# Low weight parts on VectorE, small scalings on ScalarE, and the second chunk's norm as urgent work, in the first phase of a two-layer convolution and pooling trunk

## The chip, the cores and the metric

The kernel runs on one core of a Trainium2 chip. A core has TensorE (PE: matrix products, results in eight PSUM banks), VectorE (DVE), ScalarE (ACT), GpSimd (POOL) and SyncE (SP, which here only starts DMA transfers); PEld is the loading of weights into TensorE. Each engine takes its own instructions in order, and the engines wait for each other by semaphores. The metric is the device time of one execution in microseconds (us); the median of several runs counts.

## The reference

Two residual layers on x of 1024 positions by 1024 channels. Each sub-layer is an RMS norm, a shift and a scale computed from a conditioning vector c (adaLN), the sub-layer's work, a gate and the residual sum. Layer 0 mixes tokens by a Conformer convolution, layer 1 by pooling over trailing windows; a SwiGLU block follows each. The part that the change touches is the start of layer 0:

```python
c_act = jax.nn.silu(c)
mod = c_act @ ada_w[i] + ada_b[i]                  # six vectors of 1024
sh_m, sc_m, g_m, sh_f, sc_f, g_f = jnp.split(mod, N_ADA, axis=-1)
h = rms_norm(x, norm_mix_g[i]) * (1.0 + sc_m) + sh_m
u = h @ w1 + b1                                    # 1024 -> 2048
a, g = jnp.split(u, 2, axis=-1)
u = a * jax.nn.sigmoid(g)
u = causal_depthwise_conv(u, w_dw) + b_dw          # width 31, per channel
u = jax.nn.silu(layer_norm(u, ln_g, ln_b))
y = u @ w2 + b2
x = x + (1.0 + g_m) * y
```

All data is float32, and the products must have float32's precision.

## The kernel before, in words

**Layout.** Channels lie on the 128 partitions in KT = 8 tiles, positions on the free axis. The 1024 positions are two chunks of 512: A is x[0], B is x[1]. A is worked on ahead of B, and B's convolution input reuses the last 30 columns of A's (`uhalo`).

**Products in three parts.** A float32 operand is split into a high part in the fast type fp32r and a low part, the rest. `products` (L416) multiplies high by high, high by low and low by high. One product of a weight tile with 512 columns is one matmul; a half tile ("a" or "g", 8 channel tiles times 3 parts) is 24 matmuls, a tile 48. `load_weight` (L402) makes the two parts of a weight tile of 128x1024: a DMA into `raw` (4 buffers), the high part by a cast on ACT, and the low part in one of two ways. Without `summed` it is raw - high by a TENSOR_TENSOR on DVE or POOL, whichever `either` (L151) reckons free first by the planner's clocks and prices. With `summed` ACT writes the negated high rounding and a DMA from POOL's queue adds the source to it. High and low parts share nine buffers of the tag "w" (W_BUFS), in which the first phase also keeps its modulation weights.

**First phase** (L1270 to L1375). For each channel tile k of A: two rows of the modulation matrix (`ada_pair`, L1300) come in by DMA; two dot products on DVE with silu(c) (`ada_dot`, a SCALAR_TENSOR_TENSOR with an accumulator, tile `adaw`) give the scale's and the shift's column of tile k; `gain_of` (L1310) turns the first into the norm's gain (`gains`, one column) and a TENSOR_SCALAR adds the bias to the second (`mod`), both on DVE. Then t = x * gain * 1/rms on DVE, hhi = t + shift on ACT (fp32r), hlo = the rest on DVE one round later. The weights of the first FIRST = 4 tiles of w1 for this k are one tile of 128x1024 (`w1k`), split by `load_weight` with `either`. PE multiplies: 8 matmuls each of high weight by hhi, low weight by hhi, high weight by hlo, into the eight banks `first`. So there are eight rounds of 24 matmuls. The order on DVE is bound by hand with `behind_that` (L1306); the order of the loads on SP by `load_next` (L144), which chains each load to the one before.

Behind the rounds the two weights of tile 4 are loaded and split (`early`, L1378), then all eight tiles of x for B are loaded (L1379). `conv_glu` (L579) empties the eight banks: a sigmoid on ACT, a product on DVE, `u`.

**Units, tasks and the planner.** What follows is a list of units that `run_units` (L537) emits in order: products on PE, in the order written, and loads of weights ahead of them as buffers allow. Work of the other engines is cut into tasks (L208), generators that `pace` (L185) steps each time a quarter of a tile (12 matmuls) has been emitted. The planner keeps a clock per engine: 512 columns of a matmul count 0.216 us, an operation on DVE or POOL its price. A step of an urgent task is emitted at normal priority and as soon as its time has come; a step of another task only while DVE's or POOL's clock is less than 4 us ahead of PE's, at a lower priority, and behind the products emitted so far (`step`, L175). A task may ask to be left alone for a time, in the planner's us (LOAD, L50): "late" 11.0, "load" 4.8. Within an engine the final order comes from the tool that schedules by priority and its own timing; only PE keeps the written order.

**The units here.** In this order (L1417 on): `ada_first` starts `ada_columns` (L359), which computes the other four modulation vectors of layer 0 on PE. It loads rows in pairs (2 x 512 KB) into two buffers, waits "late" ahead of the first pair and "load" ahead of the others, multiplies (`ada`, 8 matmuls a row), and loads the next pair; sixteen pairs in all. Then the task `norm_b` (L1424): B's eight squares on ACT summed on DVE into a PSUM bank (`Squares`, L462), the sum over partitions by 8 small matmuls (`var`), three Newton steps for the root on DVE (`mean_rsqrt`, L437), its spreading by 8 matmuls (`rstd`), and for each of eight tiles t, hhi and hlo (`modulated`, L509). It is not urgent and stands at the front of the task list. Then the convolution's taps for A's tiles 0 to 3: tap by tap on DVE (`ca`, in PSUM) or on ACT and POOL (`pr`, `pa`). Then tile 4 of A; then tiles 5 and 6 of A, `finish(norm_b)`, and tiles 5 and 6 of B with the same weights; then tile 7 of both, tiles 0 to 3 of B, A's layer norm, the second product `y`, and so on to the feed-forward parts.

Of the kernel before, what the change touches and what calls it, by code (L numbers as in the profile page):

```python
# [9 lines left out]
F32 = mybir.dt.float32  # L10
F32R = mybir.dt.float32r
I32 = mybir.dt.int32
AF = mybir.ActivationFunctionType
ALU = mybir.AluOpType
MUL, ADD, SUB = ALU.mult, ALU.add, ALU.subtract

P = 128
D = 1024
S = 1024
KT = D // P  # L20
# [20 lines left out]
FIRST = 4  # L41
# [5 lines left out]
PHTAPS = 29  # L47
PHLEN = 135
OUT_B = 3
LOAD = {"load": 4.8, "late": 11.0, "slow": 18.0, "next": 4.0}  # L50
AHEAD = 4
STRETCH = 1.35
LATER = 300
WARM = (22, 10, 6)
PREPARED = 120
PLAIN = 4
UNTIL = (16, 16, 20)
# [55 lines left out]
def trunk(ctx, tc, xT, c, vec, ada, adan, w1, w2, wgu, wdn, wpl, wph, out):  # L113
    nc = tc.nc
    ctx.enter_context(tc.manual_schedule(engines={mybir.EngineType.PE}))
    clock = {"PE": 0.0, "V": 0.0, "G": 0.0, "S": 0.0}
    V_ = Engine(nc.vector, "V", clock, PRICES["V"], lambda i: order(i))
    G_ = Engine(nc.gpsimd, "G", clock, PRICES["G"], lambda i: order(i))
    S_ = Engine(nc.scalar, "S", clock, PRICES["S"], lambda i: order(i))
# [11 lines left out]
    def order(ins):  # L131

        if behind[0] and last_mm[0] is not None:
            tc.add_manual_dep(ins.ins, last_mm[0], edge, reason="behind the products")
        return ins
# [8 lines left out]
    def load_next(dst, src):  # L144

        d = nc.sync.dma_start(dst, src)
        if last_load[0] is not None:
            tc.add_manual_dep(d.ins, last_load[0], edge, reason="loads in order")
        last_load[0] = d.ins.name

    def either(n):  # L151

        now = clock["PE"]
        v, g = (max(clock[e], now) + engines[e].price("tensor_tensor", n) for e in "VG")
        return V_ if v <= g else G_
# [9 lines left out]
    def nm(s):  # L165
        uid[0] += 1
        return f"{s}_{uid[0]}"
# [40 lines left out]
    class Task:  # L208
# [6 lines left out]
        def step(self, e):  # L215
            if e != "V" or self.done or clock["PE"] < self.until and not forced[0]:
                return False
            try:
# [3 lines left out]
                if said == "wait":  # L222
                    return False
                if said in LOAD:
                    self.until = clock["PE"] + LOAD[said]
                elif said is not None:
# [18 lines left out]
    def bank(name):  # L245
        return ps.tile([P, 512], F32, tag="mm", name=nm(name))
# [27 lines left out]
    x = [[cst.tile([P, ch.n], F32, name=f"x_{ch.i}_{k}") for k in range(KT)] for ch in chunks]  # L274
# [21 lines left out]
    def V(name, j, n=1):  # L296
        b = _COLS[name] + j
        return vecs[:, b : b + n]

    mod = cst.tile([P, DEPTH * 6 * KT], F32, name="mod")  # L300
    gains = cst.tile([P, 4, DEPTH * KT], F32, name="gains")
    scale_m, scale_f, gate_m, gate_f = (gains[:, i] for i in range(4))
# [96 lines left out]
        return mod[:, b : b + 1]  # L399


    def load_weight(src, n=D, load=nc.sync.dma_start, summed=False):  # L402
        raw = raws.tile([P, D], F32, tag="raw", name=nm("raw"))[:, :n]
        as_src = lambda t: t if len(src.shape) == 2 else t.rearrange("p (a b) -> p a b", a=src.shape[1])
        load(as_src(raw), src)
        hi, lo = (wts.tile([P, D], F32R, tag="w", name=nm("w"))[:, :n] for _ in range(2))
        S_.copy(hi, raw)
        if summed:
            S_.activation(lo, raw, AF.Copy, scale=-1.0)
            order(nc.gpsimd.dma_start(as_src(lo), src, accum_op=ADD))  # L410
            clock["G"] = max(clock["G"], clock["PE"]) + 1.0
            return hi, lo
        either(n).tensor_tensor(lo, raw, hi.bitcast(F32), op=SUB)
        return hi, lo

    def products(out, wt, k, act, first, last, o=0, n=None):  # L416
# [117 lines left out]
    def unit(emit, *weights):  # L534
        units.append((weights, emit))
# [138 lines left out]
    class Phased:  # L674
# [5 lines left out]
        def load(self):  # L680
            self.w = []
            for g in range(PH):
                for h in range(2):
                    t = slot(A, "wph", F32)
                    nc.sync.dma_start(t, wph[self.i, g][:, h * 512 : h * 512 + 512])
                    self.w += [t[:, m * P : m * P + P] for m in range(SHIFTS // 2)]
# [301 lines left out]
    class Pair:  # L988
# [15 lines left out]
        def prepare(self):  # L1004
# [10 lines left out]
            def fresh():  # L1015
                t = wts.tile([P, D], F32R, tag="w", name=nm("w"))
                return t[:, FRONT], t[:, BACK]
# [3 lines left out]

            with tc.high_priority(offset=-PREPARED):
                w11, w12, w22 = fresh(), fresh(), fresh()
# [30 lines left out]
    class Downs:  # L1054
# [13 lines left out]
        def load(self, dp):  # L1068
# [5 lines left out]
            wt = wts.tile([P, D], F32R, tag="w", name=nm("w")).rearrange("p (s f d) -> p s f d", s=2, f=2)  # L1074
            with tc.high_priority(offset=-PREPARED):
                S_.copy(wt[:, 0], raw)
# [212 lines left out]
    summed = V_.last.ins.name  # L1289
# [4 lines left out]
    S_.activation(ccols[:, :, 0], V("c", 0, KT), AF.Silu)  # L1294
    scale_b = cst.tile([P, KT], F32, name="scale_b")
    G_.tensor_scalar(scale_b, V("ada_b", KT, KT), 1.0, None, op0=ADD)
    ada_m = ada.rearrange("(l j k) p d -> l k p j d", l=DEPTH, j=6)
    w1k = w1[0:FIRST].rearrange("a b p (k m) -> k p (a b) m", k=KT)

# [6 lines left out]
    def behind_that(name, reason):  # L1306
        tc.add_manual_dep(V_.last.ins, name, edge, reason=reason)
        return V_.last.ins.name

    def gain_of(k):  # L1310
        V_.tensor_scalar(scale_m[:, k : k + 1], mod[:, KT + k : KT + k + 1], scale_b[:, k : k + 1], V("norm_mix_g", k), op0=ADD, op1=MUL)

    warm(WARM[0])
    b = bank("var")
# [4 lines left out]
    ada_dot(w[1], 0, 1, 0)  # L1319
    at = behind_that(summed, "while the tensor engine sums")  # L1320
    gain_of(0)
    at = behind_that(at, "in order")
    v, t = b[:, :count], b[:, 16 : 16 + count]
    V_.tensor_scalar(v, v, EPS, None, op0=ADD)
    at = behind_that(at, "in order")
    col = tmp.tile([P, 16], F32, tag="col1", name=nm("col"), bufs=1)[:, :count]
    now(rsqrt(v, col, t))
    rooted = V_.last.ins.name
    warm(WARM[1])
    r = bank("rstd")  # L1330
    for i in range(count):
        matmul(r[:, i * P : (i + 1) * P], col[:, i : i + 1].broadcast_to([P, P]), ident, start=True, stop=True)
    warm(WARM[2])
    rstd_a = temp(A.n, "ny", 2)
    h_a = st["h", 0] = [(slot(A, "hhi"), slot(A, "hlo")) for _ in range(KT)]
    fb = [bank("first") for _ in range(BANKS)] + [spare_bank("first") for _ in range(2 * FIRST - BANKS)]
    for k in range(KT + 1):
        if 0 < k < KT:
            w = ada_pair(k)
            ada_dot(w[1], 0, 1, k)  # L1340
            behind_that(lo_last if k == 1 else t_last, "behind the tile ahead of it")
        if k > 0:
            dot = V_.last.ins.name
            if k > 1:
                V_.scalar_tensor_tensor(h_a[k - 1][1], t, mod[:, k - 1 : k], h_a[k - 1][0].bitcast(F32), op0=ADD, op1=SUB)
                if k < KT:
                    behind_that(dot, "the scalar engine's part takes that long")
            for i, (wp, a) in enumerate(((0, 0), (1, 0), (0, 1))):
                for q in range(2 * FIRST):
                    matmul(fb[q], wt[wp][:, q * P : (q + 1) * P], h_a[k - 1][a], start=k == 1 and i == 0, stop=k == KT and i == 2)  # L1350
        if k < KT:
            ada_dot(w[0], 0, 0, k)
            if k == 0:
                behind_that(rooted, "while the root is spread")
            else:
                gain_of(k)
            V_.tensor_scalar(mod[:, k : k + 1], mod[:, k : k + 1], V("ada_b", k), None, op0=ADD)
            t = temp(A.n)
            V_.scalar_tensor_tensor(t, x[0][k], scale_m[:, k : k + 1], rstd_a if k else r, op0=MUL, op1=MUL)
            t_last = V_.last.ins.name  # L1360
            S_.activation(h_a[k][0], t, AF.Identity, bias=mod[:, k : k + 1])
            if k:
                wt = load_weight(w1k[k], 2 * FIRST * P, load_next)
            else:
                first_hi = S_.last.ins.name
                raw = raws.tile([P, D], F32, tag="raw", name=nm("raw"))
                load_next(raw.rearrange("p (a b) -> p a b", a=2 * FIRST), w1k[0])
                wt = [wts.tile([P, D], F32R, tag="w", name=nm("w")) for _ in range(2)]
                S_.copy(wt[0], raw)
                S_.copy(rstd_a, r)  # L1370
                tc.add_manual_dep(S_.last.ins, first_hi, edge, reason="the first tile reads the bank")
                V_.tensor_tensor(wt[1], raw, wt[0].bitcast(F32), op=SUB)
                at = behind_that(t_last, "in order")
                V_.scalar_tensor_tensor(h_a[0][1], t, mod[:, 0:1], h_a[0][0].bitcast(F32), op0=ADD, op1=SUB)
                lo_last = behind_that(at, "in order")  # L1375
    for e in clock:
        clock[e] = max(clock.values())
    early = [load_weight(w1[FIRST, i], load=load_next) for i in range(2)]  # L1378
    for k in range(KT):  # L1379
        load_next(x[1][k], xT[:, k, B.t0 : B.t0 + B.n])  # L1380
    for p in range(FIRST):
        conv_u(A, p)
        conv_glu(A, p, fb[2 * p], fb[2 * p + 1])
# [2 lines left out]
    T = {}  # L1386
# [31 lines left out]
    def norm_first():  # L1418
        squares = Squares(B, True)
        for k in range(KT):  # L1420
            squares.add(k)
            yield
        yield from norm(B, 0, False, ("h", 1), squares=squares)
    unit(lambda take: T.__setitem__("norm_b", Task(norm_first(), False, 0)))  # L1424
    taps(A, *range(FIRST))
    for p in range(FIRST, SHARED[0]):
        conv_in((A, p))
# [158 lines left out]
```

## Time and profile before

| | before |
|---|---|
| three runs, us | 1834.56, 1834.21, 1831.17; median 1834.21 |
| the profiled execution | 1831.12, its span 1829.3 |
| mean granted clock of TensorE | 0.992 |
| busy: PE, DVE, ACT, POOL | 1781.2, 1309.1, 1028.8, 589.2 us |
| moved by DMA | 340.63 MB, 186 GB/s on average |

The chain of work that ended last lies on PE for 80% of the span, on DVE for 8% and on DMA for 6%.

How to read it: a row of the timeline gives the start and the length of a run of equal instructions in us from the span's start, then engine, line, operation, out<-in with the programs' names, and in brackets how long the engine had stood idle just before and who released it. Nearly all operations are recorded in a helper (L107, L129), so the tile names tell them apart. A row of the stages gives a stretch, its length, the busy us (and instructions) of PE, PEld, DVE, ACT and POOL, PE's granted clock, the busy share of the DMA engines and GB/s. A row of the groups has busy us, the mean ns of one instruction, and the idle time ahead of it with its releasers. Matmuls overlap by their pipeline, so the distance of two starts is what one costs PE.

### The profile page before, as it was taken

Reading aid. Unit: us, or ns where it says so; the run is one execution under the profiler, and the core shown is the slowest. Engines: PE = TensorE matmul, PEld = TensorE weight load, DVE = VectorE, ACT = ScalarE, POOL = GpSimd, SP = SyncE. Lnnn points to the kernel's source line nnn. Section 1 sums busy time; section 2 is a strip of 40 time slices with the busy share of each in tenths; the row PEclk is TensorE's granted clock in tenths of the full one; section 3 lists DMA queues with packets and bytes.
Section 4 is the critical chain, followed back from the end, with each engine's and each line's share of the span. In section 5 each row is a group of like instructions: output and inputs, shape, how many; then the busy total and the mean of one; then the engine's idle time right before and its main releaser. Section 6 shows DMA issues by size and latency. Waiting matters only on the chain.

```text
span 1829.3 us, 26250 instructions
## 1 busy us (share of the span) xinstructions
PE 1781.2 (97%) x9748; PEld 1519.4 (83%) x9748; DVE 1309.1 (72%) x2136; ACT 1028.8 (56%) x1590; POOL 589.2 (32%) x632
## 2 busy tenths in 40 slices
PE   8989999999999999999999999999999999999997
PEld 7756678888888887899997888999978889999986
DVE  8878754988766237889978458778694468887845
ACT  3655575866756455655545456555554546555543
POOL 2578722877743211311117121111151211011111
PEclk9989999999999999999999999999999999999998
DMA  8838869798887997976767887655568876655462
GB/s 271 279 116 258 228 153 216 198 234 210 221 232 181 242 223 179 255 216 199 207 179 160 203 182 169 156 139 138 145 147 201 181 167 159 189 141 135 130 141 70
DMA packets 115377, 340.63 MB, mean 186 GB/s; under 512 B 11441, under 2 KB 21809, under 8 KB 115250
## 3 DMA queue, kind: packets, MB, share of 16 engines
q1 hardware_dynamic: 76656, 222.56, 36.4%
q0 software_dynamic: 37440, 115.36, 35.2%
q8 instruction: 76, 1.25, 0.3%
q10 hardware_dynamic: 1154, 1.05, 0.2%
q14 instruction: 51, 0.42, 0.1%
HBM read 334.73 MB, written 4.19 MB: 185 GB/s over the span
## 4 chain that ended last, share of the span: by engine, by line
PE 80%; DVE 8%; DMA 6%; issue 3%; POOL 2%; ACT 2%; SPq 0%; POOLq 0%; DVEq 0%; ACTq 0%
PE gate L129 23%; PE up L129 23%; PE dn L129 22%; PE y L129 5%; DMA adaw<-in_adan_dram 3%; PE a L129 2%; PE g L129 2%; DVE t L107 1%; DVE adaw L107 1%; DMA w<-in_wdn_dram 1%; DVE hlo L107 1%; DVE x L107 1%; DVE win L107 1%; DMA w<-in_wgu_dram 1%; PE ada L129 1%
## 5 line engine op out<-in xcount | busy, mean ns | idle before, releaser
L129 PE MATMUL dn<-ghi,w 128*128 128x512 f32 (+1 forms) x1440 | 468.8, 388 | 3.4 <-DMA w<-in_wdn_dram 2.0
L107 ACT ACTIVATE w<-raw 128x1024 fp32r<-128x1024 f32 (+1 forms) x260 | 241.0, 927 | 345.3 <-PE dn L129 116.7
L107 ACT CAST w<-raw 128x1024 fp32r<-128x1024 f32 (+1 forms) x390 | 319.7, 823 | 126.5 <-PE up L129 55.3
L107 DVE SCALAR_TENSOR_TENSOR x<-dn,gains,x 128x512 f32<-128x512 f32 (+1 forms) x360 | 262.6, 734 | 80.6 <-PE dn L129 77.4
L129 PEld LDWEIGHTS dn<-ghi,w 128*128 128x128 f32 x1440 | 268.4, 188 | 56.8 <-DMA w<-in_wdn_dram 2.9
L129 PE MATMUL gate<-hhi,w 128*128 128x512 f32 (+1 forms) x1088 | 310.4, 359 | 3.9 <-DMA w<-in_wgu_dram 3.9
L129 PE MATMUL up<-hhi,w 128*128 128x512 f32 (+1 forms) x1088 | 310.1, 358 | 0.0
L129 PE MATMUL dn<-glo,w 128*128 128x512 f32 (+1 forms) x720 | 278.6, 387 | 0.9 <-POOL glo L107 0.9
L107 POOL TENSOR_TENSOR pa<-pa,pr 128x512 f32<-128x512 f32 x169 | 230.5, 1426 | 26.8 <-ACT pr L107 23.9
L1045 POOL DMA_DIRECT2D w<-in_wgu_dram x80 | 69.3, 866 | 493.3 <-ACT w L107 157.6
L129 PEld LDWEIGHTS gate<-hhi,w 128*128 128x128 f32 x1088 | 196.5, 189 | 35.6 <-DMA w<-in_wgu_dram 4.8
L129 PEld LDWEIGHTS up<-hhi,w 128*128 128x128 f32 x1088 | 196.6, 189 | 30.5
L129 PE MATMUL gate<-hlo,w 128*128 128x512 f32 (+1 forms) x544 | 195.0, 358 | 1.4 <-DVE hlo L107 1.4
L129 PE MATMUL up<-hlo,w 128*128 128x512 f32 (+1 forms) x544 | 194.6, 358 | 0.0
L410 POOL DMA_DIRECT2D w<-in_wgu_dram x96 | 86.2, 898 | 320.0 <-ACT w L107 288.1
L107 DVE TENSOR_TENSOR t<-t,up 128x512 f32<-128x512 f32 (+1 forms) x88 | 54.8, 624 | 169.6 <-PE up L129 146.7
L107 DVE SCALAR_TENSOR_TENSOR ca<-u,vecs,ca 128x512 f32<-128x512 f32 x251 | 173.4, 747 | 0.6
L129 PEld LDWEIGHTS dn<-glo,w 128*128 128x128 f32 x720 | 135.8, 189 | 23.8 <-POOL glo L107 1.2
L107 ACT ACTIVATE pr<-u,vecs 128x512 f32<-128x512 f32 x169 | 113.1, 716 | 16.1 <-POOL pa L107 9.9
L129 PEld LDWEIGHTS gate<-hlo,w 128*128 128x128 f32 x544 | 102.6, 189 | 18.0 <-DVE hlo L107 2.3
L129 PEld LDWEIGHTS up<-hlo,w 128*128 128x128 f32 x544 | 102.6, 189 | 15.6
L107 DVE TENSOR_TENSOR w<-raw,w 128x512 fp32r<-128x512 f32 (+1 forms) x123 | 85.4, 703 | 28.7 <-ACT w L107 25.7
(190 smaller groups left out, 3367.0 us busy)
## 6 DMA issues: line engine op xcount, KB each, us to landing
raw<-in_wgu_dram SPq DMA_DIRECT2D x176, 512.0 KB, 5.0
w<-in_wgu_dram POOLq DMA_DIRECT2D x96, 512.0 KB, 8.0
raw<-in_wdn_dram SPq DMA_DIRECT2D x88, 512.0 KB, 5.4
adaw<-in_ada_dram SPq DMA_DIRECT2D x64, 512.0 KB, 5.7
w<-in_wdn_dram POOLq DMA_DIRECT2D x48, 512.0 KB, 8.3
raw<-in_w_dram SPq DMA_DIRECT2D x42, 512.0 KB, 6.0
w<-in_wgu_dram POOLq DMA_DIRECT2D x80, 256.0 KB, 5.6
adaw<-in_adan_dram SPq DMA_DIRECT2D x32, 512.0 KB, 6.2
```

The source lines that it names most:

```text
L107: self.last = self.order(getattr(self.eng, name)(out, *args, **kw))
L129: last_mm[0] = nc.tensor.matmul(out, lhsT, rhs, start=start, stop=stop, **kw).ins.name
L410: order(nc.gpsimd.dma_start(as_src(lo), src, accum_op=ADD))
L1045: order(nc.gpsimd.dma_start(lo, src, accum_op=ADD))
```

## The change

It does seven things. In the first phase: the low parts of the weights of rounds 1 to 7 are made on DVE, ordered behind t, and the next round's first dot product behind them; the gain and the biased shift are computed on ACT, the gain with the product of bias and norm weight made ahead on POOL; rounds 4 to 7 each load one tile of B's x, and the other four stand between and behind the weights of tile 4; a tie of the root's first instruction to the gain of tile 0 is gone. Behind it: `norm_b` is an urgent task, and "late" is 20 instead of 11.

```diff
-LOAD = {"load": 4.8, "late": 11.0, "slow": 18.0, "next": 4.0}
+LOAD = {"load": 4.8, "late": 20.0, "slow": 18.0, "next": 4.0}
+EARLY_X = 4
...
-    def load_weight(src, n=D, load=nc.sync.dma_start, summed=False):
+    def load_weight(src, n=D, load=nc.sync.dma_start, summed=False, low=None):
...
-        either(n).tensor_tensor(lo, raw, hi.bitcast(F32), op=SUB)
+        (low or either(n)).tensor_tensor(lo, raw, hi.bitcast(F32), op=SUB)
...
     G_.tensor_scalar(scale_b, V("ada_b", KT, KT), 1.0, None, op0=ADD)
+    G_.tensor_tensor(scale_b, scale_b, V("norm_mix_g", 0, KT), op=MUL)
...
     def gain_of(k):
-        V_.tensor_scalar(scale_m[:, k : k + 1], mod[:, KT + k : KT + k + 1], scale_b[:, k : k + 1], V("norm_mix_g", k), op0=ADD, op1=MUL)
+        S_.activation(scale_m[:, k : k + 1], mod[:, KT + k : KT + k + 1], AF.Identity, bias=scale_b[:, k : k + 1], scale=V("norm_mix_g", k))
...
     gain_of(0)
-    at = behind_that(at, "in order")
     v, t = b[:, :count], b[:, 16 : 16 + count]
...
-            V_.tensor_scalar(mod[:, k : k + 1], mod[:, k : k + 1], V("ada_b", k), None, op0=ADD)
+            S_.activation(mod[:, k : k + 1], mod[:, k : k + 1], AF.Identity, bias=V("ada_b", k))
...
             if k:
-                wt = load_weight(w1k[k], 2 * FIRST * P, load_next)
+                wt = load_weight(w1k[k], 2 * FIRST * P, load_next, low=V_)
+                t_last = behind_that(t_last, "in order")
+                if k >= KT - EARLY_X:
+                    load_next(x[1][k - KT + EARLY_X], xT[:, k - KT + EARLY_X, B.t0 : B.t0 + B.n])
...
-    early = [load_weight(w1[FIRST, i], load=load_next) for i in range(2)]
-    for k in range(KT):
-        load_next(x[1][k], xT[:, k, B.t0 : B.t0 + B.n])
+    early = []
+    for i in range(2):
+        early.append(load_weight(w1[FIRST, i], load=load_next))
+        for k in range(EARLY_X + i, KT, 2):
+            load_next(x[1][k], xT[:, k, B.t0 : B.t0 + B.n])
...
-    unit(lambda take: T.__setitem__("norm_b", Task(norm_first(), False, 0)))
+    unit(lambda take: T.__setitem__("norm_b", Task(norm_first(), True)))
```

## The prediction

> **What bounds the kernel now.** I read the page first, then the busy times by stage, then the groups and the timeline of the first 70 us, and last the tensor engine's waits up to 135 us beside the chain of waits.
>
> ```profile
> span 1829.3 us, 26250 instructions
> ...
> PE 1781.2 (97%) x9748; PEld 1519.4 (83%) x9748; DVE 1309.1 (72%) x2136; ACT 1028.8 (56%) x1590; POOL 589.2 (32%) x632
> ```
> ```profile
> 26.65:68.70 42.05, 40.21 (x169) 31.36 (x170) 39.22 (x52) 14.68 (x18) 15.79 (x6) 1.00 0.89 303
> 68.70:131.65 62.95, 52.81 (x253) 38.34 (x252) 47.64 (x80) 42.40 (x63) 46.01 (x47) 0.88 0.52 148
> 131.65:264.50 132.85, 124.47 (x753) 91.86 (x753) 100.14 (x163) 81.79 (x115) 88.84 (x84) 0.99 0.78 214
> 264.50:1829.30 1564.80, 1541.13 (x8455) 1339.40 (x8455) 1103.28 (x1806) 878.95 (x1379) 433.09 (x459) 1.00 0.72 181
> ```
> The tensor engine (PE) is busy 97% of the span, and from 264.50 on 1541.13 of 1564.80 us. The change touches nothing behind that point except by what it shifts, so that part should only move in time. What can be won lies ahead of it: 1.8 us idle in the first phase, 10.1 us idle with a granted clock of 0.88 in the stage from 68.70 to 131.65, and 8.4 us idle up to 264.50.
>
> **First phase.** Seven rounds, one for each channel tile k above 0; each has 24 matmuls.
>
> ```profile
> L107 DVE SCALAR_TENSOR_TENSOR adaw<-adaw,cact 128x1024 f32<-128x1024 f32 x12 | 23.0, 1916 | 0.0
> ...
> L107 POOL TENSOR_TENSOR w<-raw,w 128x1024 fp32r<-128x1024 f32 x6 | 15.8, 2631 | 21.7 <-ACT w L107 17.8 <-DVE gains L107 3.9
> ...
> L107 DVE SCALAR_TENSOR_TENSOR hlo<-t,mod,hhi 128x512 fp32r<-128x512 f32 x7 | 5.2, 742 | 0.8 <-ACT hhi L107 0.8
> ...
> L107 DVE TENSOR_SCALAR gains<-mod,scale_b,vecs 128x1 f32<-128x1 f32 x6 | 1.6, 260 | 0.0
> L107 DVE TENSOR_SCALAR mod<-mod,vecs 128x1 f32<-128x1 f32 x6 | 1.2, 202 | 0.0
> L107 DVE DVE_READ_ACCUMULATOR adaw<-adaw,cact 128x1 f32 x12 | 0.9, 76 | 0.0
> ```
> ```profile
> 26.65 3.92 PE L129 MATMUL first<-hhi,w 128*128 128x512 f32 x16 [1.33 <-ACT hhi L107]
> ...
> 31.80 1.21 DVE L107 SCALAR_TENSOR_TENSOR adaw<-adaw,cact 128x1024 f32<-128x1024 f32 x1
> ...
> 32.69 3.92 PE L129 MATMUL first<-hhi,w 128*128 128x512 f32 x16 [0.31 <-ACT hhi L107]
> ...
> 36.45 1.97 PE L129 MATMUL first<-hlo,w 128*128 128x512 f32 x8
> ...
> 38.74 3.94 PE L129 MATMUL first<-hhi,w 128*128 128x512 f32 x16 [0.32 <-ACT hhi L107]
> ...
> 39.71 2.38 POOL L107 TENSOR_TENSOR w<-raw,w 128x1024 fp32r<-128x1024 f32 x1 [2.45 <-ACT w L107]
> 39.84 3.33 DVE L107 SCALAR_TENSOR_TENSOR adaw<-adaw,cact 128x1024 f32<-128x1024 f32 x1
> ...
> 63.84 2.36 DVE L107 TENSOR_TENSOR w<-raw,w 128x1024 fp32r<-128x1024 f32 x2 [0.18 <-ACT w L107]
> ```
> A DVE dot product takes 1.21 us at 31.80 and 3.33 at 39.84. The second starts 0.13 us behind POOL's low part (2.38 us) and ends 1.08 behind it: it stood still until POOL had done. So a low part on POOL costs DVE 2.1 us, and DVE, which has no idle time here, sets the round: 38.74 - 32.69 = 6.05 us. On DVE a low part costs 1.18 (2.36 for two). A round of DVE becomes two dots 2.42, their two accumulator reads 0.15, t and hlo 2 x 0.74, low 1.18: 5.2 us. The gains (0.26) and mod (0.20) go to ACT, which is busy 14.68 of 42.05 us; the second dot product and hlo lie between the gain's input and its reader, t lies beside mod, so neither is on the path.
>
> PE then sets the round. 16 matmuls take 36.45 - 32.69 = 3.76 us, so 24 take 5.64, 0.41 less than now. Six rounds give 2.4. The gap ahead of round 1 (1.33 at 26.65), made by the first POOL part, adds up to 1.3. I take 3.0 of the 3.7; the ends are 0 (a hop to ACT keeps a wait of the old size) and 3.7. Four x loads of 0.25 MB join the last four rounds: 1.5 to 1.75 MB in 5.64 us is some 325 GB/s in each. The rate of the whole stage is 303 at a share of 0.89, so at a full share it would be 340 (an estimate); the loads stand behind the round's own weights on SP, and the next weights wait for buffers anyway. Nothing for them, at most 1 us.
>
> **The stage from 68.70 to 131.65.** PE stops in three places.
>
> ```profile
> 82.06 0.74 PE L129 MATMUL a<-hhi,w 128*128 128x512 f32 x2 [2.06 <-DMA w<-in_w_dram]
> ...
> 86.14 1.07 PE L129 MATMUL ada<-adaw,ccols 128*32 128x256 f32 x16
> ...
> 95.93 0.75 PE L129 MATMUL ada<-adaw,ccols 128*32 128x256 f32 x8 [3.03 <-DMA adaw<-in_adan_dram]
> ...
> 98.20 1.87 PE L129 MATMUL var<-ones,acc 128*128 128x1 f32 x8
> ...
> 104.26 0.39 PE L129 MATMUL a<-hhi,w 128*128 128x512 f32 x1
> ...
> 121.71 0.48 PE L129 MATMUL a<-hhi,w 128*128 128x512 f32 x1
> ...
> 128.73 0.80 PE L129 MATMUL a<-hlo,w 128*128 128x512 f32 x1 [2.65 <-DVE hlo L107]
> ...
> 135.43 1.07 PE L129 MATMUL ada<-adaw,ccols 128*32 128x256 f32 x16
> ```
> ```profile
> 82.06 4.16 PE a L129 x10
> ...
> 162.72 5.44 PE g L129 x24
> ```
> 24 matmuls at full clock take 5.44 us (162.72), 0.227 each.
> - A's tile 5, low weight late: 2.06 of waiting, then 10 matmuls in 4.1 instead of 2.3: 3.9 lost.
> - Second pair of modulation columns: from 92.90, where the wait begins, to 104.26 are 11.4 us. In them lie a pair (1.07), the sums for B's norm (1.87 at a slow clock, about 1.0 at full: an estimate) and 12 matmuls (2.72): 6.6 lost.
> - B's tile 5, which waits for B's normalised input: from 121.71 to 135.43 are 13.7 us for 24 matmuls: 8.3 lost.
>
> Together 18.8 us, slow clock included.
>
> The third goes: as an urgent task B's norm issues its eight squares at once, ahead of taps, and its eight tiles of h directly behind the root. With the first phase ending near 65.5, tile 4 ends near 76.4 (48 x 0.227), and with sums, root and their waits (near 80) eight tiles of h at 2 x 0.74 us of DVE end near 92. B's first use comes behind tiles 5 and 6 (21.8) and three pairs (3.2), near 105. It costs DVE and ACT what it costs now, earlier. The second goes too: with "late" at 20 instead of 11 the first pair comes when the planner's clock has passed tile 5 of A (two tiles are 96 x 0.216 = 20.7), three pacing points later, when tile 5's and 6's weights have been loaded; the stage's DMA share is only 0.52. The first should shrink, since the x loads now ahead of tile 5's weights on SP are four fewer.
>
> What comes in their place is on the same path:
>
> ```profile
> 14.33 0.17 DVE L107 TENSOR_SCALAR var<-var 128x4 f32<-128x4 f32 x1 [1.14 <-PE var L129]
> ...
> 16.55 0.16 DVE L107 SCALAR_TENSOR_TENSOR col<-var,col 128x4 f32<-128x4 f32 x1
> ...
> 67.34 2.42 ACT L107 ACTIVATE t<-first,vecs 128x512 f32<-128x512 f32 x4 [1.27 <-PE first L129]
> ...
> 69.64 0.62 ACT L107 ACTIVATE acc<-x 128x512 f32<-128x512 f32 x1
> ...
> 72.52 1.05 ACT L107 CAST w<-raw 128x1024 fp32r<-128x1024 f32 x1
> ...
> 75.75 1.05 POOL L410 DMA_DIRECT2D w<-in_w_dram  x1
> ...
> 86.19 0.68 DVE L107 TENSOR_TENSOR acc<-acc,t 128x512 f32<-128x512 f32 x1
> ...
> 100.10 0.17 DVE L107 TENSOR_SCALAR var<-var 128x4 f32<-128x4 f32 x1 [8.16 <-PE var L129]
> ```
> - With the change the sums come three quarters into tile 4, 36 x 0.227 = 8.2 us behind its start (the planner wants 7 of its us behind the squares' start). The squares can start when the sigmoids (2.42) free the first bank, about 1.2 us into tile 4; eight take 5.0 (0.62 each), the last addition 0.7: ready at 6.9, 1.3 early. If two weights (four ACT passes of 1.05) go in between, 2.9 late; with four weights, 7.1 late. I take 1.5 late.
> - The root's chain takes 16.55 + 0.16 - 14.33 = 2.4 us and two hops, against 2.72 us of matmuls ahead of its reader; a tap of 0.74 slipped in makes it late. I take 0.7; 0 to 2.
> - Tile 5's low weight: its cast (72.52) competes with the urgent squares on ACT, and its accumulating DMA (75.75) was issued some 3 us later. I take 1.0; 0 if the cast leads, 5 if all squares do.
> - Slow clock behind these: 1.5; 0 to 3.
>
> ```profile
> 80.00:85.00 5.00, 2.94 (x8) 2.35 (x9) 3.96 (x7) 5.00 (x8) 3.01 (x3) 0.77 1.03 241
> ...
> 195.00:200.00 5.00, 2.39 (x17) 1.32 (x15) 4.65 (x7) 1.99 (x2) 1.87 (x3) 1.00 1.04 276
> ```
> The wait of 2.06 us near 80 brought the clock to 0.77, while around 198 PE idled 2.6 us at 1.00; so short waits sometimes cost clock, and I price half.
> The Trainium skill ("TensorE: Matmul & The Clock Gate", Part 1: The HAM clock gate) lets the clock fall only after at least one idle window of about 3.4 us. By that rule the 1.5 would be nothing and the total 1.5 us better; the row at 80 speaks against it, the one at 195 for it.
>
> New waits: 1.5 + 0.7 + 1.0 + 1.5 = 4.7 us. Each tap now queues behind the squares, the root and h on DVE; at 100.10 DVE already stood 8.16 us for the sums, a stop that shrinks to about 1, which pays for this.
>
> **Given back up to 264.50.** DVE and POOL must do A's taps in some 17 us less. From 68.70 to 264.50 DVE is busy 147.8 of 195.8 us and POOL 134.9; in 178.5 that is 83% and 76%. They fit, but in-order queues will not follow fully; the columns' pairs also end three pacing points later. I take 3.0; 0 to 9.
>
> **Sum.** -3.0 - 18.8 + 4.7 + 3.0 = -14.1 us. Span 1829.3 to 1815.2. The profiled execution took 1831.12, 1.8 more than its span, and lies 3.1 below the median of 1834.21; so 1817.0 for such an execution and 1820.1 for the median.
>
> **The rivals.**
> - The squares meet the matmul: ACT does four weights first, the sums are 7.1 late rather than 1.5, with 2 more of clock and a late h: about -6.5, 1827.7. For it: ACT is busy all 5.00 us from 80 to 85. Against: weights can be cast no faster than their buffers come free.
> - Taps become the bound: A's mean needs all taps, and they end no more than 3 us earlier than now, so nearly all is handed back at the layer norm: -2, 1832. For it: 83% busy on in-order DVE. Against: much of DVE's idle time now is waiting for PE.
> - Slower: the columns' pairs, begun later, run on into the stage where DMA is full (0.78 on average, 1.03 and 1.04 above), and PE waits for each. Price: twelve pairs of the sixteen lie behind 131.65 now, and nearly all of that stage's 8.4 idle us could be theirs. Were each to wait the 3.03 seen at 95.93, that is 36.4, 28 more: +14, 1848. It decides from about 2.2 us a pair (26.4, 18 more: the whole gain and 3.9 us). Against: the pairs stay two per tile, and behind B's tile 5 the same number is left.
> - The first phase does not get faster (hops to ACT replace what POOL cost): 3.0 less, -11, 1823.
>
> **Chances.** Forecast 0.52, squares 0.16, first phase unchanged 0.08, taps 0.15, slower 0.09. A measurement of this kernel can tell about 0.2%, 3.7 us, from no change. Faster: forecast, squares and first phase, and a fifth of the taps case, 0.79; same: the rest of taps, 0.12; slower 0.09. The forecast's own range is 1812 (no new wait, nothing handed back beyond 1 us) to 1826. To 1831 it takes in the squares case and part of the taps case; out are the rest of that and the slower one.
>
> **What would show it.** Rounds 5.65 us apart with PE no longer waiting for hhi and no TENSOR_TENSOR of w on POOL; dots of 1.21; x loads between 35 and 60 us; sums on PE near 75 us with a wait under 3; h done before 95; no wait on hlo in B's tile 5, whose first matmul comes near 105; B's tile 5 ends 15 to 18 us earlier, the convolution's second product 13 to 16. Wrong would be: rounds still 6.05; a wait above 5 us at the sums; PE waiting for columns more than 9 us in all behind 115; or a wait at the mean.

## The result, and the profile after

The changed kernel takes 1823.39 us (median of six runs, 1820.1 to 1831.74), the kernel before in the same runs 1834.02 (1831.17 to 1835.56): a ratio of 0.9946, 95% interval 0.9927 to 0.9966, so 10.6 us faster. A second set of runs of the same changed kernel (e1_after, below) gave 1823.02 against 1835.54, 0.9932 [0.9916, 0.9949]. The forecast was 1820.1, a ratio of 0.9923: inside the second interval, just below the first.

The profiled execution of the first set is its slowest (1831.74); that of e1_after took 1823.27, near the median. Both are used below, each by name. First the page of the profile after, its head:

```profile
span 1830.0 us, 26248 instructions
...
PE 1783.3 (97%) x9748; PEld 1525.4 (83%) x9748; DVE 1302.6 (71%) x2127; ACT 1035.7 (57%) x1606; POOL 569.7 (31%) x626
```

The change itself is there: POOL has 19.5 us less to do, ACT 6.9 more. The stages of the same execution (length, busy us of PE, PEld, DVE, ACT, POOL, granted clock, DMA share, GB/s):

```profile
25.80:64.00 38.20, 38.20 (x169) 31.34 (x167) 32.55 (x47) 18.84 (x30) 0.00 (x0) 1.00 1.01 351
64.00:117.00 53.00, 48.81 (x251) 37.47 (x251) 42.71 (x71) 38.52 (x56) 35.35 (x37) 0.94 0.56 152
117.00:260.00 143.00, 130.05 (x758) 96.95 (x757) 106.87 (x171) 87.12 (x123) 97.52 (x95) 0.95 0.74 206
260.00:1830.00 1570.00, 1543.73 (x8455) 1340.88 (x8454) 1104.14 (x1806) 879.11 (x1379) 433.77 (x459) 0.99 0.72 180
```

In the first phase PE has no idle time left (38.20 of 38.20), POOL nothing to do, and DVE, which had set the round, is busy 32.55. In the next stage 4.2 us of idle PE are left of 10.1. Behind it, up to 260, 13.0 are idle; before it was 8.4 in the corresponding stretch. On PE's own timeline:

```profile
25.81 3.79 PE L130 MATMUL first<-hhi,w 128*128 128x512 f32 x16
...
31.25 3.79 PE L130 MATMUL first<-hhi,w 128*128 128x512 f32 x16
...
76.71 1.87 PE L130 MATMUL var<-ones,acc 128*128 128x1 f32 x8 [4.19 <-DVE acc L108]
78.43 0.77 PE L130 MATMUL g<-hhi,w 128*128 128x512 f32 x1
...
83.54 1.05 PE L130 MATMUL rstd<-ident,col 128*128 128x128 f32 x8
84.35 0.48 PE L130 MATMUL a<-hhi,w 128*128 128x512 f32 x1
...
124.46 1.01 PE L130 MATMUL adac<-quarters,t 128*128 128x4 f32 x4 [2.13 <-ACT t L108]
125.33 0.77 PE L130 MATMUL a<-hhi,w 128*128 128x512 f32 x1
```

Rounds are 31.25 - 25.81 = 5.44 us. From 25.8 to 117 one wait is left, 4.19 for the sums of B's norm, with no wait at the root (83.54), none for tile 5's weights and none in B's tile 5. Two are new: the sums', and 2.13 for `adac`, the transposed rows of the first modulation vector.

Where the time went is best followed by marks on PE. First matmul of each, in us from the span's start:

| | before | after | e1_after | e1_after, earlier by |
|---|---|---|---|---|
| tile 4 of A | 68.5 | 64.0 | 63.1 | 5.4 |
| sums of B's norm | 98.2 | 76.7 | 75.7 | |
| second half of B's tile 5 | 131.4 | 116.6 | 115.2 | 16.2 |
| B's tile 6 | 139.3 | 125.3 | 123.6 | 15.7 |
| second product y | 251.4 | 246.9 | 241.7 | 9.7 |
| end of the span | 1829.3 | 1830.0 | 1821.5 | 7.8 |

So in e1_after 16.2 us were won by B's tile 5, and 6.5 of them handed back ahead of the second product; in after, 14.8 were won and 10.3 handed back.

### The profile page after: what moved, and what is told of

Read it like the earlier page. It is cut to its first block, busy times and chain, and to the rows that moved or that the text cites. A ratio compares the mean times of both kernels' runs of the same rounds, so it can differ in the third digit from the quotient of the medians.

```text
span 1830.0 us, 26248 instructions
## 1 busy us (share of the span) xinstructions
PE 1783.3 (97%) x9748; PEld 1525.4 (83%) x9748; DVE 1302.6 (71%) x2127; ACT 1035.7 (57%) x1606; POOL 569.7 (31%) x626
## 3 DMA queue, kind: packets, MB, share of 16 engines
q10 hardware_dynamic: 1154, 1.05, 0.2%
HBM read 334.73 MB, written 4.19 MB: 185 GB/s over the span
## 4 chain that ended last, share of the span: by engine, by line
PE 85%; DVE 6%; DMA 3%; issue 2%; ACT 2%; POOL 2%; SPq 0%; POOLq 0%; DVEq 0%; ACTq 0%
PE gate L130 23%; PE up L130 23%; PE dn L130 22%; PE y L130 5%; PE a L130 3%; PE g L130 3%; PE first L130 2%; DMA w<-in_wdn_dram 1%; DVE t L108 1%; DMA adaw<-in_adan_dram 1%; ACT w L108 1%; DVE x L108 1%; DVE win L108 1%; DMA w<-in_wgu_dram 1%; ACT t L108 1%
## 5 line engine op out<-in xcount | busy, mean ns | idle before, releaser
L108 DVE TENSOR_TENSOR w<-raw,w 128x512 fp32r<-128x512 f32 (+1 forms) x130 | 94.3, 733 | 30.8 <-ACT w L108 27.6
```

The costliest lines, as they stand in the source:

```text
L108: self.last = self.order(getattr(self.eng, name)(out, *args, **kw))
```

## The experiments

The forecast's theory: the three stops of PE in the stage behind the first phase go, and most of that stays. The rivals: the first phase alone makes nearly all of the gain (B); what is won by B's tile 5 is handed back by the fixed orders behind it, whatever is won (C); what is handed back is lost to the DMA of the modulation columns (D).

| run | median us | ratio to before [95%] | second product at |
|---|---|---|---|
| e1_after | 1823.02 | 0.9932 [0.9916, 0.9949] | 241.7 |
| e2_first_only | 1832.51 | 0.9980 [0.9965, 0.9994] | 248.5 |
| e3_not_urgent | 1828.79 | 0.9966 [0.9955, 0.9978] | 247.4 |
| e4_late11 | 1830.47 | 0.9976 [0.9963, 0.9988] | 245.7 |
| e5_sums10 | 1821.69 | 0.9921 [0.9908, 0.9935] | 239.6 |
| e5_sums12 | 1826.73 | 0.9937 [0.9919, 0.9956] | 240.2 |
| e6_rows_dve | 1830.67 | 0.9963 [0.9949, 0.9977] | 247.1 |
| e7_squares_dve | 1829.82 | 0.9962 [0.9947, 0.9977] | 248.4 |
| e8_after_cut | 1826.95 | 0.9932 [0.9911, 0.9953] | 247.2 |
| e8_before_cut | 1846.33 | 1.0040 [1.0025, 1.0055] | 268.3 |
| e9_half_columns | 1822.15 | 0.9908 [0.9886, 0.9931] | 235.6 |
| e10_rows_later | 1824.92 | 0.9928 [0.9910, 0.9946] | 246.9 |

Three groups ran on three chips, with medians of the kernel before of 1835.54 (e1 to e4), 1837.27 (e5 to e7) and 1839.14 (e8 to e10), so the ratios compare them, not the times. The second product's mark comes from one execution each.

**The changed kernel again.**

> The changed kernel once more, unaltered, for a second profile. The first profiled execution (1831.74 us) was the slowest of seven, the others took 1820.1 to 1823.9. Theory A (what was handed back is fixed by the order of the work: 4.2 us of waiting at the sums, a slow clock behind it and behind the spreading of the first modulation columns, taps at the mean): the second profile shows the same waits up to the convolution's second product, which starts some 4.7 us earlier than before. Rival (the first profile was disturbed): the second product starts 9 to 12 us earlier, and waits for modulation columns behind 120 us are shorter.

The waits at the sums (4.20), for the rows (2.13) and at the mean (0.97) are the same again, as theory A had it, and the columns' waits aren't shorter (8.5, in after 7.8). But the second product comes 9.7 us earlier than before, not 4.7: there the rival's 9 to 12 holds. The same waits go with a clock that falls in one execution and not in the other (last section), which neither theory had. The parts below are read from this execution. PE's waits up to the second product, by what is waited for (us in total, times, longest; `ada` are the products of the modulation columns, `var` the sums of B's norm, `adac` the transposing of the rows, `mean` the layer norm's mean; further down `rstd` is the spreading of a root and `vhi` an input of the second product):

```profile
PE ada L130 <- DMA adaw<-in_adan_dram: 8.5, 5, 3.3
PE var L130 <- DVE acc L108: 4.2, 1, 4.2
PE adac L130 <- ACT t L108: 2.1, 1, 2.1
PE mean L130 <- DVE acc L108: 1.0, 1, 1.0
```

**One part at a time.** First the first phase's new engines alone (x of B loaded behind it as before, "late" 11, the norm not urgent):

```diff
-LOAD = {"load": 4.8, "late": 20.0, "slow": 18.0, "next": 4.0}
+LOAD = {"load": 4.8, "late": 11.0, "slow": 18.0, "next": 4.0}
...
-                if k >= KT - EARLY_X:
-                    load_next(x[1][k - KT + EARLY_X], xT[:, k - KT + EARLY_X, B.t0 : B.t0 + B.n])
...
-    unit(lambda take: T.__setitem__("norm_b", Task(norm_first(), True)))
+    unit(lambda take: T.__setitem__("norm_b", Task(norm_first(), False, 0)))
```

> Only the first phase's arithmetic is changed (low parts on DVE, gains and shifts on ACT); B's input is loaded as before, the norm is not urgent, late is 11. Theory A: the rounds come down to 5.44 us and the first phase ends 4.4 us earlier; the three stops behind it stay, so the whole kernel gains 4.4, give or take 1.5 (ratio 0.9976). Rival B (the first phase is where nearly all of the measured 10.6 us come from, what the norm wins being handed back): 8 us or more.

Its waits on PE up to the second product:

```profile
PE ada L130 <- DMA adaw<-in_adan_dram: 9.0, 7, 3.4
PE a L130 <- DVE hlo L108: 3.8, 2, 2.6
PE a L130 <- DMA w<-in_w_dram: 3.7, 1, 3.7
```

Tile 4 began 6.0 us earlier than before, the second product 2.9: all three stops of the stage are still there. The wait for tile 5's low weight has grown from 2.06 to 3.65, since PE now reaches it earlier; the second pair of columns costs 1.9 (3.5 before), hlo the same 3.8. By the medians the first phase by itself is worth 3.0 us of the 12.5 of the whole change on the same chip. B falls. Within the first phase the low parts on DVE and the gains on ACT were not run apart.

Then the whole change without the urgency, and the whole change without the later columns:

```diff
-    unit(lambda take: T.__setitem__("norm_b", Task(norm_first(), True)))
+    unit(lambda take: T.__setitem__("norm_b", Task(norm_first(), False, 0)))
```

> The changed kernel with B's norm as an ordinary task again, all else as changed (late is 20, x loads early). Theory A: B's tile 5 waits for hlo again, 3 to 8 us, but the 4.2 us wait at the sums goes: 2 to 5 us slower than the changed kernel, 6 to 8 us faster than before. Rival B: as fast as the changed kernel, within 1.5 us, since the taps bound both.

```diff
-LOAD = {"load": 4.8, "late": 20.0, "slow": 18.0, "next": 4.0}
+LOAD = {"load": 4.8, "late": 11.0, "slow": 18.0, "next": 4.0}
```

> The changed kernel with late at 11 again, all else as changed. Theory A: the second pair of modulation columns meets the loads of tiles 5 and 6 again and PE waits some 3 us for it with a slow clock behind it: 3 to 6 us slower than the changed kernel. Rival B: no difference within 1.5 us. A third view (late only moves the spreading of the first columns, where PE now waits 2.1 us, to another place): up to 3 us faster than the changed kernel.

PE's waits without the urgency:

```profile
PE ada L130 <- DMA adaw<-in_adan_dram: 8.3, 4, 4.9
PE rstd L130 <- DVE col L108: 4.2, 1, 4.2
PE a L130 <- DVE hlo L108: 4.0, 4, 1.0
PE y L130 <- DVE vhi L108: 3.4, 1, 3.4
```

And with "late" at 11:

```profile
PE ada L130 <- DMA adaw<-in_adan_dram: 9.1, 8, 3.4
PE mean L130 <- DVE acc L108: 4.3, 1, 4.3
PE var L130 <- DVE acc L108: 4.2, 1, 4.2
PE y L130 <- DVE vhi L108: 2.2, 1, 2.2
```

Each brings back the stop that it was made for: without the urgency PE waits again for hlo in B's tile 5 (four times 1.0), with "late" at 11 the second pair of columns is late again (2.06 and 0.62 at 91.6). The urgency is worth 5.8 us of 1828.79 and the later columns 7.5 of 1830.47, against e1_after. Both are somewhat more than theory A's 2 to 5 and 3 to 6. In both, new waits stand at the layer norm's root or mean and at y (7.7 and 6.4 us). So the parts support each other: where one is missing, part of what the others win goes to the next fixed wait. Only the first phase was run alone. The loading of B's x was not taken back alone; but the wait for tile 5's weight, 3.65 where x comes late (e2_first_only), is 0.28 and none in these two, and of the parts that e2_first_only lacks the two share only the early x loads, which points to these.

**The sums' wait, moved out of the way.** The sums stand three quarters into tile 4 on PE. Let them come later, by a wait of 10 or 12.5 of the planner's us, or make every second square on DVE:

```diff
-LOAD = {"load": 4.8, "late": 20.0, "slow": 18.0, "next": 4.0}
+LOAD = {"load": 4.8, "late": 20.0, "slow": 18.0, "next": 4.0, "sums": 10.0}
...
+        yield "sums"
         yield from norm(B, 0, False, ("h", 1), squares=squares)
```

> The changed kernel with the sums of B's norm on PE held back until the planner's clock is 10 us past the squares' start: they fall behind tile 4 instead of three quarters into it, 2.7 us of matmuls later. Theory A (the 4.2 us wait at the sums and the slow clock behind it, 7.2 us in all, are the price of the place of the sums): the wait shrinks to about 1.5, 3 to 5 us faster than the changed kernel at the sums, 2 to 5 at the end. Rival C (whatever PE wins ahead of B's tile 5 is handed back behind it, the stage up to the second product being bound by modulation columns and taps): the tile starts earlier, the end is within 1.5 us of the changed kernel.

> The same with 12.5 us instead of 10: the sums fall a quarter into tile 5 of A, 5.4 us of matmuls later than in the changed kernel. Theory A: no wait and no slow clock, 6 to 8 us gained by tile 5, 3 to 7 us at the end. Rival C: within 1.5 us at the end. B's h comes some 3 us later and should still be ready for B's tile 5.

```diff
-                S_.activation(sq, x[ch.i][k], AF.Square)
+                if self.psum and k % 2:
+                    V_.tensor_tensor(sq, x[ch.i][k], x[ch.i][k], op=MUL)
+                else:
+                    S_.activation(sq, x[ch.i][k], AF.Square)
```

> The changed kernel with every second square of B on DVE instead of ACT. In the changed kernel seven weight passes of 1.05 us stand between B's squares on ACT, so the last square starts at 74.3 us, 2.9 us behind the place of the sums on PE. If ACT's queue makes the sums late (theory A), four squares fewer there bring the sums 2 to 4 us earlier, and with the slow clock 2 to 6 us by tile 5, 2 to 5 at the end. If the last x tile's arrival makes them late, nothing changes at the sums. Rival C: earlier at the sums, the end within 1.5 us.

All three do what they are for: the wait at the sums falls from 4.2 to 1.4, 0 and 0, and B's tile 5 begins 4.1, 5.4 and 6.3 us earlier than in e1_after. At B's tile 6 it is gone: 3.3 and 5.8 us later, and 1.5 earlier. PE of e5_sums12, in the middle of the second half of B's tile 5:

```profile
124.28 1.02 PE L130 MATMUL adac<-quarters,t 128*128 128x4 f32 x4 [11.41 <-ACT t L108]
```

And ACT of the same execution, ahead of that (a number in brackets is ACT's own idle time and who ended it):

```profile
118.99 0.72 ACT L108 ACTIVATE pr<-u,vecs 128x512 f32<-128x512 f32 x1 [0.49 <-POOL pa L108]
120.21 0.72 ACT L108 ACTIVATE pr<-u,vecs 128x512 f32<-128x512 f32 x1 [0.50 <-POOL pa L108]
121.42 0.69 ACT L108 ACTIVATE t<-g,vecs 128x512 f32<-128x512 f32 x1 [0.49 <-POOL pa L108]
122.64 1.33 ACT L108 ACTIVATE pr<-u,vecs 128x512 f32<-128x512 f32 x2 [0.53 <-POOL pa L108]
123.88 0.35 ACT L108 COPY t<-ada 128x256 f32<-128x256 f32 x1
```

PE waits 11.4 us for a copy of 0.35 us. It stands on ACT behind tap products, and each of these waits for POOL's sum of the tap before (0.72 + 0.49 = 1.21 us a tap); POOL does nine such sums without a break, 11.26 us from 113.78 on. In e5_sums10 and e7_squares_dve the same copy costs 6.58 and 6.46 us. e7_squares_dve then lost 4.25 at the layer norm's root and 3.43 at y, and its ratio is 0.9962 against 0.9932; e5_sums10 kept 2.1 us at the second product. Of theory A's gains at the end, none shows in e5_sums12 (0.9937) or e7_squares_dve. C fits what is won beyond the change: it meets the next instruction in a fixed queue. Of what the change itself won, 9.7 of 16.2 stayed. e5_sums10 has the best ratio of the versions that compute everything, but its interval overlaps the changed kernel's: they aren't told apart.

**The copy on another engine.**

```diff
-        S_.copy(rows, acc[:, :Q])
+        V_.tensor_copy(rows, acc[:, :Q])
```

> The changed kernel with the copy of the modulation rows from PSUM on DVE instead of ACT. In the changed kernel the first copy (0.36 us) stands on ACT behind two weight passes that wait for a buffer which PE frees only at the end of B's tile 5; PE waits 2.13 us for it and DVE 5.1. Theory A: that wait goes, 1.5 to 3 us faster than the changed kernel. Rival C: no difference within 1.5 us.

The wait of 2.13 is gone and B's tile 6 begins 2.9 us earlier than in e1_after, but the columns' two waits are 3.73 and 4.64 long and the mean's is 5.39: the second product comes 5.4 later. A miss as a repair. And the copy no longer waited for: with everything behind it a task of its own, the rows in a tile of their own, and the sums at 12.5:

```diff
+        if j == 2:
+            Task(spread_columns(j, rows), False, 0).free = True
+            return
...
+    def spread_columns(j, rows):
+        if j == 2:
+            yield "rows"
```

> The kernel with the sums a quarter into tile 5, and the spreading of the first modulation columns on PE as a task of its own 16 us later by the planner's clock, so that PE does not stand for the late copy (11.4 us there). If that wait were itself the loss, the second product would start 8 to 11 us earlier than with the sums alone, and the kernel be some 10 us faster than the changed one. If it only shows the lag of ACT's queue (theory C), the wait turns up elsewhere, at the sigmoids' banks, the mean or the columns, and at most 4 us are won.

B's tile 6 came at 116.9, 6.8 earlier than in e1_after; then the columns cost 12.4 us, the rows of the next vector 3.68, and the second product was 5.2 later. That is C's case: the 11.4 us wait was not itself the loss.

**Less work for the taps.** In both kernels ten taps of A's tiles are left out:

```diff
-            self.next, self.acc, self.part, self.busy = 0, None, None, 0
+            self.next, self.acc, self.part, self.busy = (0 if ch.i else 10), None, None, 0
```

> The changed kernel with the first ten of the 31 taps left out for A's tiles that are not done on PE (work left out). In the kernels with later sums the copy of the modulation rows on ACT came 6.6 and 11.4 us late, behind tap products (pr) that go to and fro with POOL at 1.24 us a tap. Theory C (taps on ACT and POOL hand back part of the gain): without these taps the changed kernel's waits for the rows (2.1) and at the mean (1.0) go and the second product starts 3 to 6 us earlier than in the changed kernel. Theory D (only the modulation columns' loads hand it back): within 1.5 us at the second product.

> The kernel before with the same ten taps left out: the control. Its stops (weights of tile 5, second pair of columns, B's h) do not hang on the number of taps as such, though h shares DVE with them. Theory C: the second product 0 to 4 us earlier than before, less than the same cut brings in the changed kernel. If it brings as much or more here, the taps are not what the change ran into.

With less to do both kernels reached the second product later (247.2 against 241.7, 268.3 against 251.4): the rest of the work came in another order (in the changed kernel the layer norm's mean stood on PE 6.5 us earlier, and 31.3 us ahead of the second product instead of 19.4), and PE waited 8.3 us for columns and 2.5 for the mean in the changed kernel, 16.6 and 3.6 in the one before. A miss for each theory: the runs leave open what DVE's capacity is worth, and show only that fewer taps do not of themselves shorten PE's waits.

**Half the columns' bytes.** Each pair of modulation rows brings 512 KB instead of 1 MB, and the second half of the columns is computed from the first:

```diff
-        src = lambda j, k: adan[k, :, (j - 2) * D : (j - 1) * D]
+        src = lambda j, k: adan[k, :, (j - 2) * D : (j - 2) * D + D // 2]
```

> The changed kernel with only half of each row of the four modulation vectors loaded (256 KB instead of 512; the two other quarters multiply the same half again, so the modulation is wrong in them). In the changed kernel PE waits 8.5 us in all for these loads behind B's tile 5, and the clock falls behind one of the waits. Theory D: these waits go and the second product starts 6 to 10 us earlier. Theory C: half of it or less, as rows and mean come late instead.

PE's waits behind the sums, up to the second product:

```profile
PE ada L130 <- DMA adaw<-in_adan_dram: 2.5, 1, 2.5
PE adac L130 <- ACT t L108: 2.1, 1, 2.1
PE mean L130 <- DVE acc L108: 1.9, 1, 1.9
```

The columns' waits fall from 8.5 to 2.5, and the second product is 6.1 earlier. D is right in that the columns' DMA is the largest wait left there. It isn't the answer to what the change handed back: before, these waits behind B's tile 5 were 6.3 already. The median shows less of it (0.9908, with an interval that overlaps that of e1_after): behind the second product this execution took 1584.7 us, that of e1_after 1579.8.

## Why the prediction was right, and by how much its terms were off

The direction, the mechanism and the range were right: PE's three stops went, and the median lies 3.3 us above the forecast. That it lies so near is partly luck: the first phase won more than forecast and three other terms lost more, and in the executions read the sum is 6.3 off, nearer to the squares rival's -6.5 than to the forecast. The forecast of -14.1 for the span stands against -7.8 between the executions of before and of e1_after, by its own terms:

| term | forecast | e1_after | how read |
|---|---|---|---|
| first phase | -3.0 | -5.4 | 68.5 to 63.1 |
| three stops | -18.8 | -17.9 | what the other terms leave of -16.2 |
| new waits | +4.7 | +7.1 | below |
| handed back ahead of y | +3.0 | +6.5 | 16.2 to 9.7 |
| behind y | 0 | +1.9 | 1577.9 to 1579.8 |
| sum | -14.1 | -7.8 | |

The medians differ by more than these two executions, by 10.6 and 12.5: the execution of before was 3.1 below its median, that of e1_after 0.25 above. How the terms lie in a median execution isn't shown.

**First phase: right, too small.** PE sets the round, as forecast. But 24 matmuls behind one another take 5.44 us, and the forecast took 5.64, from 16 that had followed a wait of 0.31, though it read the 5.44 itself further on (162.72). Seven rounds from 25.81 to 64.05 give 38.24 against 41.85 before, 3.6 of it; the rest is the start of round 1 (24.84 in e1_after, 26.65 before). The x loads cost nothing to be seen: the phase moves 351 GB/s at a share of 1.01 and PE never waits.

**Stops: right.** None of the three is left. B's tile 5 begins at 108.5, not near 105 as said, since the new waits ahead are longer; its second half begins 16.2 earlier and B's tile 6, behind it, 15.7, where 15 to 18 were forecast for its end. The dot products now take 1.22 us each (1.21 forecast).

**New waits: the right place, too small.** The sums were to be 1.5 late (2.9 with two weights in between); they were 4.2 late. ACT of e1_after shows why:

```profile
64.57 1.06 ACT L108 CAST w<-raw 128x1024 fp32r<-128x1024 f32 x1
65.52 1.08 ACT L108 ACTIVATE w<-raw 128x1024 fp32r<-128x1024 f32 x1
66.47 1.16 ACT L108 ACTIVATE t<-x 128x512 f32<-128x512 f32 x2
...
69.41 2.19 ACT L108 ACTIVATE t<-x 128x512 f32<-128x512 f32 x4
71.49 1.04 ACT L108 CAST w<-raw 128x1024 fp32r<-128x1024 f32 x1
72.43 1.07 ACT L108 ACTIVATE w<-raw 128x1024 fp32r<-128x1024 f32 x1
73.39 1.04 ACT L108 CAST w<-raw 128x1024 fp32r<-128x1024 f32 x1
74.32 0.64 ACT L108 ACTIVATE t<-x 128x512 f32<-128x512 f32 x1
```

The last square (74.32) stands behind seven passes over weights of 1.05 each (the two left out here, at 67.51 and 68.46, are a cast and a negation too), where the squares rival had eight. That rival had the mechanism, and the forecast's term was too small by it; its whole price (7.1 late) didn't come. Behind the wait the clock fell: the sums took 1.72 us to the next matmul and the 12 of g 5.11 up to the root (after, 76.71 to 83.54), where e5_sums12, without the wait, needed 0.81 and 2.82. That is 3.2, against 1.5; in e1_after 2.9, with the wait 7.1. The waits at the root and for tile 5's weight (0.7 and 1.0) didn't come: PE came there later itself.

**Handed back: the step that was mis-sized.** 3.0 was a guess between 0 and 9, argued from DVE's and POOL's load; the second product was to come 13 to 16 us earlier and comes 9.7 (in after 4.5). DVE's load doesn't show as the cause: in e1_after it is busy 97.97 of the 124.70 us from 117 to the second product, 79% (before, from 131.65, 77%), and stands idle 5.08 us waiting for PE. POOL's part isn't settled (73%, before 70%): its sums of taps hold ACT in e5_sums12. ACT of e1_after:

```profile
120.84 1.06 ACT L108 ACTIVATE w<-raw 128x1024 fp32r<-128x1024 f32 x1 [0.74 <-PE g L130]
121.80 1.03 ACT L108 CAST w<-raw 128x1024 fp32r<-128x1024 f32 x1
122.73 0.36 ACT L108 COPY t<-ada 128x256 f32<-128x256 f32 x1
```

ACT's copy of the rows, for which PE waits 2.13 and DVE with it, stands behind two passes over weights, and these had waited until PE freed a buffer. From 115.2 to 123.6 this costs 1.5 against before (the pair of columns that before had in this stretch, 1.0, comes later now). From B's tile 6 to the second product e1_after takes 118.1 us and before 112.1. The groups on PE in that stretch, of before:

```profile
L129 PE MATMUL ada<-adaw,ccols 128*32 128x256 f32 x176 | 13.0, 388 | 6.4 <-DMA adaw<-in_adan_dram 6.3
L129 PE MATMUL pc<-uph,wph 128*128 128x128 f32 x64 | 7.7, 278 | 0.0
```

and of e1_after:

```profile
L130 PE MATMUL ada<-adaw,ccols 128*32 128x256 f32 x192 | 13.9, 388 | 8.5 <-DMA adaw<-in_adan_dram 8.5
L130 PE MATMUL pc<-uph,wph 128*128 128x128 f32 x64 | 9.3, 315 | 0.0
```

Of the 6.0, 0.9 are the pair that comes later (16 matmuls more), 2.2 the columns' waits, 1.0 the mean's wait, and 1.6 `pc` (the taps of tile 7, done on PE) at a slow clock, 0.75 from 185 to 190, behind the longest of the columns' waits (3.35). A wait at the mean had been named as what would show the forecast wrong, as had columns' waits above 9 behind 115: the mean waits 1.0, the columns 8.5. The taps case and the columns case each had a small part. The split rests on one execution of each kernel. That no single wait is the loss is what e6_rows_dve and e10_rows_later show: with a wait taken away, others grew. That the order of the queues sets the total fits them, and e5_sums12 and e7_squares_dve too, but no run changed that order alone.

**Behind the second product: not constant.** The forecast let the part from 264.50 on only move. In the executions seen it took 1578 to 1585 us, also with nothing changed between: 1579.8 in e1_after and 1583.1 in after. Of these 3.3 us, 2.4 are idle time of PE (it is busy 1554.12 in e1_after and 1555.04 in after), as much as its waits for down-projection weights differ (1.6 and 4.0 in the whole execution); why they differ wasn't tried.

## What to carry to other kernels

When PE is nearly always busy and a stop is taken out, ask which instruction PE will then reach too early, and what stands ahead of its producer in that engine's order: here a copy of 0.36 us held PE for 2.1 to 11.4 us. Being urgent among the tasks did not put the squares ahead of the weights' casts on ACT, so count the passes that can come between urgent steps. Try the parts of such a change together as well as alone: of the 6.0 us that the first phase alone had won by tile 4, 2.9 were left at the second product.

## What the runs showed of the hardware

The clock fell behind the sums' wait (4.19 and 4.20 us) in both executions of the changed kernel (0.65 and 0.50 from 75 to 80 us), and behind a wait of 2.13 us in one execution and not in the other, at the same place of the same kernel. After, then e1_after, the 5 us behind that wait (granted clock is the third number from the end):

```profile
125.00:130.00 5.00, 5.00 (x14) 4.03 (x14) 4.42 (x8) 2.78 (x6) 4.92 (x7) 0.50 0.86 214
```
```profile
125.00:130.00 5.00, 5.00 (x36) 3.64 (x34) 4.96 (x8) 2.99 (x5) 4.92 (x6) 1.00 0.61 131
```

The first 24 matmuls of B's tile 6 took 8.4 us (125.33 to 133.70) against 5.6 (123.62 to 129.24): 2.8 us of the 5.2 by which the second product differs between the two. The Trainium skill ("TensorE: Matmul & The Clock Gate", Part 1: The HAM clock gate) gives a window of about 3.4 us that runs freely, and a fall after a whole idle one; that the same wait hits or misses agrees with a window that runs freely, that 2.13 us are enough does not agree with a whole idle one. Nor does the longer wait always cost more: one of 2.75 us in before (ending at 200.15) left the clock at 1.00 in the 5 us behind it, one of 2.46 in e9_half_columns (ending at 180.29) brought 0.66.

A wait costs PE more than its length also without a slower clock: 16 matmuls behind a wait of 0.31 took 3.76 us (32.69 to 36.45, before), 16 without one 3.63 (25.81 to 29.44, after).
